# Rows of the experts' weights read in pairs, score products by turns on the two halves of TensorE's rows, and two more places for weights in each experts' stage

## The chip, the cores and the metric

One core of one Trainium2 chip. The time is device microseconds of one execution; runs are told as a median with the lowest and the highest. Smaller is better. All data are float32; matmuls take float32 or the fp32r type, and TensorE's two clock levels are 2.4 GHz (a granted clock of 1.00 in the views) and 1.2 GHz (0.50).

## The reference

The kernel computes a first block (a Fourier and state-space mixer over 256 tokens and 256 context tokens) and then two layers of a second block, on tokens of width 1024. Cut to what the change touches:

```python
for l in range(2):
    sh1, sc1, g1, sh2, sc2, g2 = split(silu(c) @ ada_w[l] + ada_b[l], 6)   # the same for the context from c_ctx
    h = rms_norm(x, norm_mix[l]) * (1 + sc1) + sh1
    # l == 0: even_layer (4 heads of differential attention, 8 of neighbourhood attention with a bias, all 64 wide)
    # l == 1: odd_layer  (8 heads of latent attention, 4 heads of retention in both directions)
    y, yc = layer(h, hc)
    x = x + g1 * y
    h2 = rms_norm(x, norm_ffn[l]) * (1 + sc2) + sh2
    x = x + g2 * expert_choice_ffn(h2, moe_router[l], moe_w1[l], moe_w3[l], moe_w2[l])
    # in layer 0 the context tokens go through the same experts' stage

def expert_choice_ffn(h, w_router, w1, w3, w2):        # 16 experts, width 1024, hidden width 1024
    aff = softmax(h @ w_router)
    gate, idx = top_k(swapaxes(aff, 1, 2), 32)          # each expert takes 32 of 256 tokens
    xe = h[bidx, idx]
    hid = silu(xe @ w1) * (xe @ w3)
    ye = (hid @ w2) * gate
    return zeros_like(h).at[bidx, idx].add(ye)
```

The three matrices of an expert are 4 MiB each, 192 MiB per layer, and each is used once.

## The kernel before, in words

One program runs the stages one after the other; inside a stage a scheduler decides the order of instructions on each engine from the order in which generators emit them (`weave` interleaves two generators, for instance one that attends with one that projects).

**The experts' stage** (`moe`, its `run` at the end of each layer). For expert `e`, `ffn` multiplies the 32 (layer 1) or 64 (layer 0: 32 of x and 32 of the context) chosen tokens by `moe_w1`, `moe_w3` and, after `silu` and a product, `moe_w2`. Each matrix comes as four loads of 1 MiB, each issued by SyncE (SP) in `load_m` (line 1253): a load takes 256 rows of the matrix, that is two blocks of 128 along the contraction, into a tile `wm` of 128 partitions by 2048 values. Partition p gets row p of the first block and row p of the second, two runs of 4 KB that lie 512 KB apart in HBM:

```python
w = pool.tile([128, 2048], F32, name="wm", tag=tag).rearrange("p (k n) -> p k n", k=2)
sv = src.rearrange("(k p) n -> p k n", p=128)
nc.sync.dma_start(w, sv[:, k0:k0 + 2])
```

The place of a load comes from a list, `slots`: a first round (`first`, which also holds places that are needed later for gathered tokens, the `xf` tiles) and then `all`, over and over. In layer 0 `all` has 16 places and the first round 20; in layer 1 they are 20 and 22. Places called `wx` come from the pools `mx0` (2), `mx1` (6) and others. A load into a place waits for the last matmul that read what was there; SP issues loads in order, so all later loads wait with it.

**The contraction's order.** Block k of the contraction holds channels 128k to 128k+127 everywhere: in the gathered tokens (`gather`: a product of the tokens' columns `xp` with a matrix `P` of zeros and ones), in the transposes of `hid` for the third matrix, in the transposes in `route` that feed the router, in the router's rows (`router_rows`), in the modulation columns (`ada`, sections 6 to 9, whose results are turned into columns) and in the columns of `norm_ffn_2` and `ada_b_2`.

**The scores.** In `even_attend` a score product contracts over 64 values, so it uses one half of TensorE's 128 rows: the two halves of a head pair lie on partitions 0 to 63 and 64 to 127. `scores` emits one head's products into one PSUM bank; with a bias (neighbourhood attention) the bias is added by a product of full height with a constant matrix `flipm`, behind the first score product. `retention` has three such groups: the state (`rv,kw`, 64 columns wide), the scores (`rqT,rkT`) and the cross term (`sst,rqT`). In the views line 149 is the helper that issues all matmuls, line 256 the one that transposes by a matmul with `kb`'s identity.

**Memory.** `kb` holds constants (identity, `tri`, `flipm`, `iota1`), `CV` columns and, later, the router's rows and affinities. POOL's own DMA descriptors have an area of 16384 bytes per partition.

Of the kernel before, what the change touches and what calls it, by code (L numbers as in the profile page):

```python
# [27 lines left out]
OP = mybir.AluOpType  # L28
# [8 lines left out]
def _constants():  # L37
# [9 lines left out]
    base = np.concatenate([ident, tri.reshape(128, 512), flip, iota1], 1)  # L47
# [45 lines left out]
    even = np.concatenate([np.tile(c64, (2, 1)), np.tile(s64, (2, 1)), perm, na.reshape(128, 128)], 1)  # L93
# [20 lines left out]
def kernel(ctx, tc, A, out, dbg=None):  # L114
# [130 lines left out]
    kb = pers.tile([128, 800], F32, name="kb")  # L245
    ident = kb[:, 0:128]
    tri = kb[:, 128:640].rearrange("p (a b) -> p a b", a=4)
    flipm = kb[:, 640:768]
    iota1 = kb[:, 768:800]
# [14 lines left out]
    CV = pers.tile([128, 200], F32, name="CV")  # L264
# [12 lines left out]
    hT = [htp.tile([128, 8, 512], F32R, name=f"hT{i}") for i in range(2)]  # L277
    pro = ExitStack()
# [4 lines left out]
    v4 = pp.tile([128, 128], F32, name="v4")  # L283

# [55 lines left out]

    def vcol(name, i):
        c = VCI[name] + i
        return VC[:, c:c + 1]
# [14 lines left out]

    def ada(src, s, pair, cols, bias, between=None, bank=None, ws=None):

        p = (bank or psa)()
        for b in range(2):
# [149 lines left out]
    with tc.issue_after(after):  # L512
        late_rows()
    now(c2)
# [539 lines left out]
    AFF = [CV[:, 128 + 32 * s:160 + 32 * s].rearrange("p (t e) -> p t e", t=2) for s in range(2)]  # L1054
    RW = [CV[:, 0:128].rearrange("p (k n) -> p k n", k=8), RWC]

    def router_rows(l):
        nc.sync.dma_start(RW[l], A["moe_router_2"][l].rearrange("(k p) n -> p k n", p=128))
# [22 lines left out]
    def route(l, s, src, at="a", tag="b", jt="b"):  # L1081
# [62 lines left out]
    def moe(l, streams, stk):  # L1144
# [42 lines left out]
        def gather(s, part, k, n=1):  # L1187
# [3 lines left out]
            if k % n == 0:  # L1191
                c = slice(128 * k, 128 * k + 128 * n)
# [49 lines left out]
        def load_m(src, k0, apart=False):  # L1242
# [5 lines left out]
            sv = src.rearrange("(k p) n -> p k n", p=128)  # L1248
            if apart:
                for k in range(2):  # L1250
                    nc.sync.dma_start(w[:, k], sv[:, k0 + k])
            else:
                nc.sync.dma_start(w, sv[:, k0:k0 + 2])
# [578 lines left out]
```

## Time and profile before

| | |
|---|---|
| time, median of 3 runs | 1906.96 us (1906.41 to 1912.91) |
| the profiled execution's own time | 1906.99 us |
| its span, first to last instruction | 1905.1 us (1.9 us lie around it) |
| mean granted clock of TensorE | 0.922 |
| busy: TensorE, VectorE, ScalarE, GpSimd | 1652.3, 794.4, 519.3, 335.1 us |
| loads of experts' weights | 382 of 1024 KB, median 18.4 us from issue to landing |

The span is the time from the first to the last instruction; what follows refers to microseconds from its start. A busy TensorE (PE) is not one at its peak, since matmuls are pipelined and their ends are modelled. The "DMA share" of a window is the mean busy share of the core's 16 DMA engines (packets that overlap make it a little over 1), GB/s what they moved. The chain of waits goes back from the last instruction to what released each step.

### The profile page before, as it was taken

The numbers are of one execution on the slowest core, as the hardware profiler recorded it, in microseconds if no ns is written. First come the engines' busy times: TensorE is split into PE (matmuls) and PEld (weight loads), VectorE is DVE, ScalarE is ACT, GpSimd is POOL, SyncE is SP. The second block draws the span as 40 slices with busy tenths as digits, with TensorE's granted clock in tenths as the row PEclk, the third lists the DMA queues.
The fourth block names the chain that finished last, engine by engine and source line by source line (L and its number), as shares of the span: only waits on it lengthen the run. The fifth ranks groups of instructions, "written<-read, shape, count | busy, mean of one in ns | idle before, by whom it ended". The sixth has DMA issues, their size and how long they took to land.

```text
span 1905.1 us, 29062 instructions
## 1 busy us (share of the span) xinstructions
PE 1652.3 (87%) x12036; PEld 1026.2 (54%) x12036; DVE 794.4 (42%) x1563; ACT 519.3 (27%) x1042; POOL 335.1 (18%) x288
## 2 busy tenths in 40 slices
PE   5999999899999998999989997789998966666665
PEld 4877777799887676433323322278784522222221
DVE  4538798947546655322323121164743300000002
ACT  4335555636443442211200000062532200000001
POOL 3114553633413310000000000041300000000001
PEclk8999999999999999999999999999997976776767
DMA  9576544555576539899989999951397999999996
GB/s 343 198 233 219 173 148 141 170 190 190 186 235 168 187 139 382 300 373 409 409 338 409 409 409 409 402 163 71 126 352 273 408 408 409 409 409 409 409 409 274
DMA packets 223016, 557.11 MB, mean 292 GB/s; under 512 B 23531, under 2 KB 80199, under 8 KB 222884
## 3 DMA queue, kind: packets, MB, share of 16 engines
q1 hardware_dynamic: 216608, 547.92, 76.9%
q10 hardware_dynamic: 5732, 6.26, 1.0%
q8 instruction: 95, 1.56, 0.3%
q0 software_dynamic: 544, 1.06, 0.1%
q14 instruction: 37, 0.30, 0.0%
HBM read 554.16 MB, written 1.05 MB: 291 GB/s over the span
## 4 chain that ended last, share of the span: by engine, by line
PE 60%; DMA 26%; DVE 8%; ACT 3%; issue 2%; POOL 1%; SPq 0%; DVEq 0%; POOLq 0%; ACTq 0%
PE ps_a L149 48%; DMA wm<-in_moe_w_dram 22%; PE ps_b L149 7%; PE ps_b L256 3%; DMA w<-in_w_in_dram 2%; DVE w L800 1%; PE ps_g L149 1%; DMA w<-in_w_ada_dram 1%; DVE wh L205 1%; ACT wh L203 1%; DMA w<-in_w_out_dram 1%; DVE ye L1323 1%; DVE pr L1404 1%; DVE hid L1305 1%; DVE acc L614 1%
## 5 line engine op out<-in xcount | busy, mean ns | idle before, releaser
L149 PE MATMUL ps_a<-wm,xf 128*32 128x256 f32 (+1 forms) x1792 | 280.0, 558 | 73.6 <-DMA wm<-in_moe_w_dram 71.8
L149 PE MATMUL ps_a<-wm,hidT 128*32 128x256 f32 (+1 forms) x1536 | 211.8, 529 | 47.4 <-DMA wm<-in_moe_w_dram 31.7
L149 PEld LDWEIGHTS ps_a<-wm,xf 128*32 128x32 f32 (+1 forms) x1792 | 90.4, 138 | 255.9 <-issue 133.3
L203 ACT ACTIVATE wh<-w 128x1024 fp32r<-128x1024 f32 (+3 forms) x152 | 151.7, 1007 | 164.6 <-PE ps_a L149 99.9
L1305 DVE TENSOR_TENSOR hid<-hid,ps_a 128x512 f32<-128x512 f32 (+1 forms) x32 | 17.7, 555 | 375.2 <-PE ps_a L149 375.2
L205 POOL TENSOR_TENSOR wh<-w,wh 128x1024 fp32r<-128x1024 f32 (+3 forms) x50 | 116.0, 2321 | 304.4 <-ACT wh L203 278.5
L205 DVE TENSOR_TENSOR wh<-w,wh 128x1024 fp32r<-128x1024 f32 (+3 forms) x102 | 135.2, 1329 | 71.9 <-ACT wh L203 71.4
L149 PEld LDWEIGHTS ps_a<-wm,hidT 128*32 128x32 f32 (+1 forms) x1536 | 70.4, 133 | 158.6 <-issue 74.8
L1323 DVE TENSOR_TENSOR ye<-ps_a,SC 32x512 f32<-32x512 f32 (+1 forms) x128 | 70.8, 553 | 193.9 <-PE ps_a L149 192.3
L1303 ACT ACTIVATE hid<-ps_a 128x512 f32<-128x512 f32 (+1 forms) x32 | 15.7, 490 | 480.9 <-PE ps_a L149 458.8
L149 PE MATMUL ps_a<-hT,wh 128*128 128x512 f32 (+1 forms) x672 | 136.3, 359 | 6.6 <-ACT hT L496 5.0
L1222 POOL TENSOR_TENSOR Pg<-Pg,CV 128x128 f32<-128x128 f32 x24 | 9.5, 421 | 748.7 <-DVE Pg L1220 748.7
L149 PEld LDWEIGHTS ps_a<-hT,wh 128*128 128x128 f32 x672 | 110.9, 197 | 25.9 <-ACT hT L496 5.4
L149 PE MATMUL ps_a<-E,wh 128*128 128x256 f32 x768 | 102.3, 288 | 6.1 <-DVE wh L205 2.5
L149 PE MATMUL ps_a<-wm,xe 128*32 128x256 f32 (+1 forms) x768 | 104.3, 481 | 0.7 <-ACT hid L1303 0.5
L149 PEld LDWEIGHTS ps_a<-E,wh 128*128 128x128 f32 x768 | 95.1, 192 | 12.6 <-issue 3.2
L149 PE MATMUL ps_a<-wh,E 128*128 128x256 f32 (+1 forms) x576 | 100.9, 326 | 0.1
L149 PEld LDWEIGHTS ps_a<-wh,E 128*128 128x128 f32 x576 | 81.5, 188 | 12.6 <-issue 5.0
L149 PE MATMUL ps_a<-wm,ye 128*32 128x256 f32 x512 | 51.6, 543 | 25.5 <-DMA wm<-in_moe_w_dram 25.5
L614 DVE SCALAR_TENSOR_TENSOR acc<-ps_a,CV,acc 128x189 f32<-128x189 f32 (+2 forms) x160 | 66.7, 427 | 8.2 <-ACT acc L603 5.7
L1023 ACT ACTIVATE pr<-ps_a,nb 128x512 f32<-128x512 f32 (+1 forms) x80 | 48.0, 601 | 76.0 <-DVE nb L1020 63.8
L149 PE MATMUL ps_a<-w,SC 128*32 128x128 f32 x1728 | 64.4, 281 | 2.7 <-DMA w<-in_w_ada_dram 2.1
(525 smaller groups left out, 2416.4 us busy)
## 6 DMA issues: line engine op xcount, KB each, us to landing
wm<-in_moe_w_dram SPq DMA_DIRECT2D x382, 1024.0 KB, 18.4
w<-in_ada_w_dram SPq DMA_DIRECT2D x46, 1024.0 KB, 5.8
w<-in_even_w_in_dram SPq DMA_DIRECT2D x24, 1024.0 KB, 6.4
w<-in_w_ada_dram SPq DMA_DIRECT2D x12, 1024.0 KB, 8.9
w<-in_w_in_dram SPq DMA_DIRECT2D x8, 1024.0 KB, 7.4
w<-in_even_w_out_dram SPq DMA_DIRECT2D x8, 1024.0 KB, 6.8
w<-in_w_in_dram SPq DMA_DIRECT2D x12, 512.0 KB, 7.3
w<-in_w_in_dram SPq DMA_DIRECT2D x8, 768.0 KB, 4.4
```

The source lines that it names most:

```text
L149: PE.matmul(o, l, r, start=start, stop=stop, **kw)
L203: S.activation(hv, wv, AF.Copy)
L205: (G if flip_lo[0] == 0 else V).tensor_tensor(lo, wv, hv, op=OP.subtract)
L256: PE.transpose(o, i, ident[:n, :n])
L614: V.scalar_tensor_tensor(o, xi[:, r0 + dr:r1 + dr, c0 + dc:c1 + dc], tap(i, j), o, op0=OP.mult, op1=OP.add)
L800: V.scalar_tensor_tensor(w[:, r], cb[:, c, 1], dt[:, c, 24 + h:25 + h], w[:, r], op0=OP.mult, op1=OP.add)
L1023: S.activation(pr[:, :n], ps[:, :n], AF.Exp, bias=nb, scale=scale, accum_out=su)
L1222: G.tensor_tensor(g_, g_, bcast(AFF[s][:, t, e4, None], [128, 4, 32]), op=OP.mult)
L1303: S.activation(hid, p1[:, :N], AF.Silu)
L1305: V.tensor_tensor(hid, hid, p3[:, :N], op=OP.mult)
L1323: V.tensor_tensor(ye[o:o + 32, s, N * j:N * j + N], py[i:i + 32, :N], G2[i:i + 32, :], op=OP.mult)
L1404: V.scalar_tensor_tensor(pr[0][0][:, :n], pr[1][0][:, :n], rc, pr[0][0][:, :n], op0=OP.mult, op1=OP.add)
```

## The change

1. **Rows in pairs.** A load of 256 rows now gives partition p rows 2p and 2p+1 of the 256: one run of 8 KB in HBM. Block k of the contraction so holds every second channel (`in_pairs`). Everything on the contraction's side follows: the transposes in `route` and of `hid`, the gathered columns (read with a step of 2 where `xp` is made, in layer 1, or where it is used as stationary operand, in layer 0), the moving operand of `ada` in sections 6 to 9, the router's rows and the columns of `norm_ffn_2` and `ada_b_2` (a new function `pair_rows`: three more DMAs on POOL, two transposes, three copies on VectorE).
2. **Two more places** in each experts' stage: `mx0` has 4 instead of 2, `mx1` 8 instead of 6, so `all` has 18 and 22 places and the first rounds 22 and 24. Room for them comes from the descriptor area (1024 instead of 16384 bytes per partition); besides, `CV` moves to the pool of `hT`, `flipm` from `kb` to `ke`, the affinities to `BC` and the first router's rows to `tri`.
3. **Scores by turns.** `scores` emits both halves of a head pair in turn, into two PSUM banks, the biases first; the three groups of `retention` go by turns on the halves too.

```diff
-            sv = src.rearrange("(k p) n -> p k n", p=128)
+            sv = src.rearrange("(m p i) n -> p m i n", p=128, i=2)[:, k0 // 2]
...
-                nc.sync.dma_start(w, sv[:, k0:k0 + 2])
+                nc.sync.dma_start(w, sv)
...
+    def in_pairs(j, n=128):
+        c = 256 * (j // 2) + j % 2
+        return slice(c, c + 2 * n - 1, 2)
...
+    def pair_rows():
+        ab = A["ada_b_2"]
+        ab = ab if len(ab.shape) == 2 else ab.rearrange("o l n -> (o l) n")
+        for l in range(2):
+            rows_in(v5, 8 * l, ab[l:l + 1, 3072:5120].rearrange("o (m c) -> (o m) c", c=256))
+        rows_in(v5, 16, A["norm_ffn_2"].rearrange("l (m c) -> (l m) c", c=256))
+        p = psb()
+        for i in range(2):
+            tr(p[:, 24 * i:24 * i + 24], v5[:, i::2])
...
-                    mm(p[32 * j:32 * j + 32, 0:128], SC[:, 4 * b + k, pair, :], w[:, k, 128 * j:128 * j + 128],
+                    mm(p[32 * j:32 * j + 32, 0:128], SC[:, 4 * b + k, pair, :],
+                       w[:, k, in_pairs(j) if paired else slice(128 * j, 128 * j + 128)],
...
-                tr(p[:, 256 * j + 128 * t:256 * j + 128 * t + 128],
-                   src[:, t, (2 * kk + j) * 128:(2 * kk + j + 1) * 128])
+                tr(p[:, 256 * j + 128 * t:256 * j + 128 * t + 128], src[:, t, in_pairs(2 * kk + j)])
...
-                    c = 128 * (k % n)
-                    mm(ps, pair[s][i][:, t, c:c + 128], Ps[s][:, t], start=t == 0 and i == 0, stop=t == 1 and i == 1)
+                    c = slice(0, 128) if n == 1 else in_pairs(k % n)
+                    mm(ps, pair[s][i][:, t, c], Ps[s][:, t], start=t == 0 and i == 0, stop=t == 1 and i == 1)
...
-                    tr(pt[:, 128 * c:128 * c + 128], hid[:, 128 * c:128 * c + 128])
+                    tr(pt[:, 128 * c:128 * c + 128], hid[:, in_pairs(c)])
...
-        def scores(ps, kind, ch, half, qs, bias=None):
-            hs_ = slice(64 * half, 64 * half + 64)
+        def scores(kind, ch, qs, bias=None):
+            pss = [psa(), psa()]
+            hs_ = [slice(64 * c, 64 * c + 64) for c in range(2)]
+            for c in range(2 if bias is not None else 0):
+                mm(pss[c][:, 0:256], flipm, bias[c], stop=False)
             for i, kv in enumerate(KVs):
-                b = bias is not None and i == 0
-                o = ps[:, 256 * i:256 * i + 256]
-                mm(o, Q[hs_, 4 * kind + ch, qs], kv[hs_, kind, 256 * ch:256 * ch + 256], stop=not b)
-                if b:
-                    mm(o, flipm, bias, start=False)
+                for c in range(2):
+                    mm(pss[c][:, 256 * i:256 * i + 256], Q[hs_[c], 4 * kind + ch, qs],
+                       kv[hs_[c], kind, 256 * ch:256 * ch + 256], start=i > 0 or bias is None)
+            return pss
...
-        for h in range(4):
-            o, a_ = slice(64 * (h % 2), 64 * (h % 2) + 64), h // 2
-            ps = psa()
+        for a_ in range(2):
+            pss = [psa(), psa()]
             for j in range(2):
-                mm(ps[:, 256 * j:256 * j + 256], rkT[o, a_, 128 * j:128 * j + 128], rqT[o, a_, :])
-            V.tensor_tensor(D[:, h], ps, D[:, h], op=OP.mult)
-            yield
+                for par in range(2):
+                    o = slice(64 * par, 64 * par + 64)
+                    mm(pss[par][:, 256 * j:256 * j + 256], rkT[o, a_, 128 * j:128 * j + 128], rqT[o, a_, :])
...
-    mx = enter(ms, name="mx0", bufs=2, reuse_waits="tile")
+    mx = enter(ms, name="mx0", bufs=4, reuse_waits="tile")
...
-    mx = enter(ms, name="mx1", bufs=6, reuse_waits="tile")
+    mx = enter(ms, name="mx1", bufs=8, reuse_waits="tile")
...
-    nc = _bacc.Bacc("TRN2", target_bir_lowering=False, num_devices=1)
+    nc = _bacc.Bacc("TRN2", target_bir_lowering=False, num_devices=1, dynamic_dma_scratch_size=1024)
```

Three places of the instructions' order. First SP's queue from where the first experts' stage is loaded (`wm<-in_moe_w_2_dram` is a load of 1 MiB of experts' weights, `kb<-in_moe_router_dram` the second layer's router, `in_ada_w_dram` modulation weights), as a difference of the two:

```order
-L1253 DMA wm<-in_moe_w_2_dram 128x2x1024 x6
-L1058 DMA kb<-in_moe_router_dram 128x8x16
-L1253 DMA wm<-in_moe_w_2_dram 128x2x1024
+L1279 DMA wm<-in_moe_w_2_dram 128x2048 x8
+L1085 DMA kb<-in_moe_router_dram 128x4x32
+L1279 DMA wm<-in_moe_w_2_dram 128x2048
 L189 DMA w<-in_ada_w_dram 128x4x512 x2
-L1253 DMA wm<-in_moe_w_2_dram 128x2x1024 x183
-L1251 DMA wm<-in_moe_w_2_dram 128x1024 x2
+L1279 DMA wm<-in_moe_w_2_dram 128x2048 x181
+L1277 DMA wm<-in_moe_w_2_dram 128x1024 x2
```

Eight instead of six loads stand ahead of the router's rows, 181 instead of 183 behind the last modulation weights, and each is one run per partition where it was two.

Second PE's queue in the neighbourhood attention of x (`KV,Q` is a score product on one half of the rows, `nb_t,kb` and `nb_t,ke` the bias product on all rows, `kb,pr` transposes of the probabilities). Before:

```order
L149 MATMUL ps_a<-KV,Q 128x256
L149 MATMUL ps_a<-nb_t,kb 128x256
L256 MATMUL ps_b<-kb,pr 128x128 x4
L149 MATMUL ps_a<-KV,Q 128x256 x2
L149 MATMUL ps_a<-nb_t,kb 128x256
L149 MATMUL ps_a<-KV,Q 128x256
```

After:

```order
L149 MATMUL ps_a<-nb_t,ke 128x256
L149 MATMUL ps_a<-KV,Q 128x256 x2
L255 MATMUL ps_b<-kb,pr 128x128 x4
L149 MATMUL ps_a<-nb_t,ke 128x256
L149 MATMUL ps_a<-KV,Q 128x256 x2
```

The bias now comes ahead of a head's two score products, which follow each other; both lie on the same half.

Third PE's queue at the context's attention, which is woven into projections of x (`E,wh`; the products `Q,ke` turn queries, `KV,prT` apply probabilities). Before, one of the single score products:

```order
L149 MATMUL ps_a<-KV,Q 128x256
L256 MATMUL ps_b<-kb,pr 128x128 x2
L149 MATMUL ps_a<-E_4479,wh 128x256
L149 MATMUL ps_a<-E_4480,wh 128x256
L149 MATMUL ps_a<-E_4479,wh 128x256 x2
```

After, one of the pairs:

```order
L149 MATMUL ps_a<-E_4489,wh 128x256
L149 MATMUL ps_a<-KV,Q 128x256 x2
L149 MATMUL ps_a<-E_4489,wh 128x256
L149 MATMUL ps_a<-E_4490,wh 128x256
L149 MATMUL ps_a<-E_4489,wh 128x256 x2
```

In this stretch 32 score products stood in 25 places of the queue; now they stand in 18, of which 14 are a product on the lower half and one on the upper half side by side.

## Rows read from the trace of the kernel before

**Rows 1.** The span in 40 equal slices: GB/s moved by DMA

```profile
GB/s 343 198 233 219 173 148 141 170 190 190 186 235 168 187 139 382 300 373 409 409 338 409 409 409 409 402 163 71 126 352 273 408 408 409 409 409 409 409 409 274
```

**Rows 2.** The chain that ended last, shares of the span

```profile
PE 60%; DMA 26%; DVE 8%; ACT 3%; issue 2%; POOL 1%; SPq 0%; DVEq 0%; POOLq 0%; ACTq 0%
PE ps_a L149 48%; DMA wm<-in_moe_w_dram 22%; PE ps_b L149 7%; PE ps_b L256 3%; DMA w<-in_w_in_dram 2%; DVE w L800 1%; PE ps_g L149 1%; DMA w<-in_w_ada_dram 1%; DVE wh L205 1%; ACT wh L203 1%; DMA w<-in_w_out_dram 1%; DVE ye L1323 1%; DVE pr L1404 1%; DVE hid L1305 1%; DVE acc L614 1%
```

**Rows 3.** Stages: length, busy us (xcount) by engine, clock, DMA share, GB/s

```profile
467.00:590.00 123.00, 121.70 (x1182) 104.33 (x1182) 61.61 (x157) 52.48 (x133) 41.25 (x42) 1.00 0.62 201
592.00:735.00 143.00, 139.44 (x899) 103.80 (x898) 93.63 (x193) 59.81 (x135) 40.65 (x34) 0.99 0.57 186
982.00:1237.00 255.00, 222.88 (x964) 72.22 (x960) 49.09 (x79) 8.96 (x15) 4.83 (x12) 1.00 1.03 408
957.00:982.00 25.00, 21.15 (x87) 7.11 (x89) 6.61 (x12) 1.19 (x2) 0.00 (x0) 0.86 0.71 277
1340.00:1372.00 32.00, 31.82 (x216) 23.92 (x215) 22.55 (x37) 13.84 (x32) 15.93 (x17) 1.00 0.20 68
1437.00:1453.00 16.00, 15.44 (x96) 9.46 (x100) 5.48 (x12) 4.82 (x9) 2.09 (x2) 0.50 0.43 136
1459.00:1889.00 430.00, 301.15 (x3095) 121.22 (x3090) 52.92 (x133) 24.06 (x60) 3.66 (x9) 0.75 1.02 407
```

**Rows 4.** SP's waits, 790 to 1090 us: total, times, longest

```profile
SPq L1253 <- PE ps_a L149: 199.4, 95, 18.3
```

**Rows 5.** PE's waits for weights, 1095 to 1240 us: total, times, longest

```profile
PE ps_a L149 <- DMA wm<-in_moe_w_dram: 17.0, 26, 1.2
```

**Rows 6.** The same, 1459 to 1889 us

```profile
PE ps_a L149 <- DMA wm<-in_moe_w_dram: 112.0, 117, 2.9
```

**Rows 7.** PE's timeline, scores: start us, us, engine, line, operation, count

```profile
473.71 0.70 PE L149 MATMUL ps_a<-KV,Q 64*128 64x256 f32 x4
...
496.32 0.70 PE L149 MATMUL ps_a<-KV,Q 64*128 64x256 f32 x2
...
623.03 0.70 PE L149 MATMUL ps_a<-KV,Q 64*128 64x256 f32 x2
623.66 0.70 PE L149 MATMUL ps_a<-nb_t,kb 128*128 128x256 f32 x2
...
655.37 1.14 PE L149 MATMUL ps_a<-KV,Q 64*128 64x256 f32 x8
```

**Rows 8.** PE's timeline, retention's state and first scores

```profile
1346.12 2.57 PE L149 MATMUL ps_a<-rv,kw 128*64 128x128 f32 x32
1348.62 1.13 PE L149 MATMUL ps_a<-rqT,rkT 64*128 64x256 f32 x4
```

**Rows 9.** POOL's timeline, a DMA of the late rows

```profile
20.22 0.51 POOL L287 DMA_DIRECT2D v<-in_norm_ffn_dram  x1
```

**Rows 10.** Weight loads of TensorE by tile: busy us, mean ns

```profile
L149 PEld LDWEIGHTS ps_a<-P,xp 128*128 128x128 f32 x128 | 19.9, 224 | 13.9 <-issue 10.6 <-ACT xp L1201 1.4 <-ACT xf L163 0.8
L256 PEld LDWEIGHTS ps_t<-kb,hid 128*128 128x128 f32 x64 | 6.7, 141 | 19.7 <-DVE hid L1305 19.7
```

**Rows 11.** DMA, 350 to 354 us, rows of 1 KB: packets, MB, share

```profile
q1 hardware_dynamic: 1444, 1.46, 109.6%
```

**Rows 12.** DMA, 327 to 331 us, rows of 2 KB

```profile
q1 hardware_dynamic: 805, 1.62, 105.1%
```

**Rows 13.** DMA, 1040 to 1060 us, rows of 4 KB

```profile
q1 hardware_dynamic: 2121, 8.19, 102.6%
```

**Rows 14.** DMA queues of instruction packets, whole span: packets, MB, share

```profile
q8 instruction: 95, 1.56, 0.3%
q14 instruction: 37, 0.30, 0.0%
```

**Rows 15.** DMA, 1560 to 1564 us, one instruction packet

```profile
q14 instruction: 1, 0.01, 0.5%
```

**Rows 16.** DMA, 960 to 964 us, one instruction packet

```profile
q8 instruction: 1, 0.02, 1.5%
```

More of the change, by code (lines that the diff above doesn't have):

```diff
@@ L277 @@
     hT = [htp.tile([128, 8, 512], F32R, name=f"hT{i}") for i in range(2)]
+    CV = htp.tile([128, 200], F32, name="CV")
     pro = ExitStack()
@@ L283 @@
     v4 = pp.tile([128, 128], F32, name="v4")
+    v5 = pp.tile([24, 256], F32, name="v5")
     def rows_in(t, r0, ap, eng=G):
@@ L357, in ada_early @@
             early[l, s].append(w)
+    def in_pairs(j, n=128):
+        c = 256 * (j // 2) + j % 2
+        return slice(c, c + 2 * n - 1, 2)
     def ada(src, s, pair, cols, bias, between=None, bank=None, ws=None):
         p = (bank or psa)()
+        paired = pair == 1 and 6 <= s < 10
         for b in range(2):
@@ L1344 @@
     l3 = enter(el3, name="el3", bufs=1, reuse_waits="tile")
-    ke = l2.tile([128, 768], F32, name="ke")
+    ke = l2.tile([128, 896], F32, name="ke")
     S.dma_start(ke, A["k_even"])
@@ L1393, in even_attend @@
             for h in range(4):
-                pr = []
-                for c in range(2):
-                    ps = psa()
-                    scores(ps, 0, h, c, qs)
-                    pr.append(softmax_p(l2, ps, n, 1.0, "pr"))
+                pr = [softmax_p(l2, ps, n, 1.0, "pr") for ps in scores(0, h, qs)]
                 rc = sm.tile([128, 1], F32, name="rc", bufs=6)
@@ L1417, in even_attend @@
             su8 = sm.tile([128, 8], F32, name="su8")
-            for h in range(8):
-                ps = psa()
-                scores(ps, 1, h // 2, h % 2, qs, None if nb_t is None else nb_t[:, t, h])
-                pr, su = softmax_p(l2, ps, n, 1.0, "pr")
-                G.tensor_copy(su8[:, h:h + 1], su)
-                values(po[:, 64 * h:64 * h + 64], transposed(l2, pr, nk), 1, 64 * h)
-                yield
+            for hh in range(4):
+                prs = [softmax_p(l2, ps, n, 1.0, "pr")
+                       for ps in scores(1, hh, qs, None if nb_t is None else [nb_t[:, t, 2 * hh + c] for c in range(2)])]
+                for c, (pr, su) in enumerate(prs):
+                    h = 2 * hh + c
+                    G.tensor_copy(su8[:, h:h + 1], su)
+                    values(po[:, 64 * h:64 * h + 64], transposed(l2, pr, nk), 1, 64 * h)
+                    yield
             V.reciprocal(su8, su8)
@@ L1714, in retention @@
             cr = rs_.tile([128, 2, 2, 2, 128], F32, name="cr")
[L1715 to L1721 removed]
+            pss = [psa(), psa()]
+            for a_ in range(2):
+                for d in range(2):
+                    c = 128 * (2 * d + a_)
+                    for par in range(2):
+                        o = slice(64 * par, 64 * par + 64)
+                        mm(pss[par][:, c:c + 128], rqT[o, a_, qs], sst[o, d, a_, :])
+            for par in range(2):
+                ps = pss[par]
                 dq = dec[:, 0, t].rearrange("p d (a b) -> p d a b", b=2)[:, :, :, par, None]
@@ L1780 @@
     x3 = enter(x3s, name="x3b", bufs=2, side="right", reuse_waits="tile")
[L1781 removed]
+    slots["all"] += [(mx, "wx")] * 8 + [(ml, "wx")] * 4 + [(hring, "wh"), (hring, "wi")] * 2 + [(ring, "w")] * 4 + [(x3, "wx")] * 2
     slots["first"] += slots["all"]
```

52 lines of the change are left out of this document (26 added, 26 removed).

## The prediction

> **What bounds the kernel now.** I read the chain of waits first [rows 2]: 60% of the span hangs on TensorE (PE) and 26% on DMA, of which 22%, some 420 us, are loads of experts' weights. Then GB/s by slices [rows 1]: two flat stretches at 409 between lower values, so weights come at one constant rate there, while elsewhere DMA has room. The windows by stage [rows 3] say what each stage waits for. The attention stretches (467 to 590 and 592 to 735 us) have PE busy for 99% and 98% of the time with DMA at 0.62 and 0.57: every PE microsecond saved there ends the stage earlier. From 982 to 1237 us and from 1459 to 1889 us DMA's share is 1.03 and 1.02: there only fewer or cheaper packets help, or loads that have landed before. That PE has room is seen in its waits for weights: 17.0 us at the end of the first experts' stage [rows 5], 112.0 us in the second [rows 6]. A load of 1 MiB costs 2.56 us there (8.19 MB in 20 us, [rows 13]).
>
> Ahead of both stretches lies a gap in DMA: 0.71 from 957 to 982 us, 0.43 from 1437 to 1453 us [rows 3]. SP then waits for PE to give a place back: 199.4 us in 95 waits between 790 and 1090 us [rows 4]. So the last load ends, in both stages, at "when DMA resumes, plus 2.56 us for each load still to come".
>
> **The change part by part.**
>
> *Places.* With two more, the load that goes out into a given freed place is two further on in the list, so when DMA resumes two loads fewer are left. The gaps have room for them: 0.29 of 25 us is 7.3 us, 0.57 of 16 us is 9.1 us, and two loads take 5.1 us. So -5.1 us in each stage, -10.2 us. Below, nothing, if another wait takes the gap; above, 9.1 us in the second stage.
>
> *Rows in pairs.* A load moves the same bytes in half as many data packets, 8 instead of 16 per DMA engine. No row shows an 8 KB packet of this queue, so I bound its price from three sides. First, shorter rows of the same queue, as busy time of 16 engines per packet's bytes: 1 KB took 1.096 x 64 us / 1.46 MB, 0.049 us [rows 11]; 2 KB took 0.085 us [rows 12]; 4 KB took 0.164 us [rows 13]. Two halves cost more than the whole by 2 x 0.049 - 0.085 = 0.013 us, and by 2 x 0.085 - 0.164 = 0.006 us. An 8 KB packet should then cost 0.328 us less 6 to 13 ns; I take 8 ns, close to the nearer pair, so 8 x 8 = 64 ns per load. Second, no gain at all, if a long run is cut into pieces of 4 KB. Third, instruction packets: those of q14 hold 8 KB each (0.30 MB in 37, [rows 14]) and one took 0.5% of 64 us, 0.32 us, by rounding 0.29 to 0.35 [rows 15], on both sides of 0.328; those of q8 hold 16 KB and one took 1.5%, 0.96 us [rows 16], against 0.656 for four of 4 KB. By their name these carry instructions, not tiles, so I go by the queue's own rows. Loads that gain: 255 us / 2.56, less the two, some 98 in the first stage (-6.3 us), and 430 / 2.56 less two, 166, in the second (-10.6 us); -16.9 us. Bounds: 0 and -27 us for 13 ns, and a loss, below. PE's 17.0 us of waiting in the first stage [rows 5] cover the 11.4 us that DMA gives up there.
>
> The Trainium skill ("DMA: Bandwidth & Descriptors", section "Why small descriptors are slow") puts a fixed cost of about 3 cycles on each packet, beside one cycle per 32 bytes. By that, an estimate, two packets of 131 cycles become one of 259, 1.1% of 2.56 us or 0.03 us per load, and the sum would be 9 us smaller in gain (1883 us). The rows above give 2.5% and decide here.
>
> *Scores of the context* (467 to 590 us). A product is two records. One on one half alone (x2 at 496.32 us) and two on different halves side by side (x4 at 473.71) both show 0.70 us [rows 7], of which 0.63 pass until the successor starts (623.03 to 623.66): the second is free. The queue has 18 such places instead of 25: -7 x 0.63 = -4.4 us, on a stage that is PE's. Bounds -6 and 0 (if softmax becomes late: two heads' scores now need two PSUM banks at once).
>
> *Scores of x* (592 to 735 us). Neighbourhood attention stood as score, bias, score: 3 x 0.63 = 1.88 us [rows 7]. Two products on one half, beside two on the other, take 1.14 us shown, 1.07 to the successor (x8 at 655.37), so a further product of 256 columns adds 0.43 to 0.63, and each change between half and full height costs the other 0.2 us. Bias, score, score has one change less, 1.68 us. But where before both heads stood together (score, bias, two scores side by side, bias, score: 5 x 0.63 = 3.14 us), the new order on the same half gives 2 x 1.68 = 3.36 us. By the order, summed over the 16 heads and the differential scores, I get 39.0 us before and 38.3 us now: -0.7 us, bounds -3 and +1.
>
> *Retention.* Two score products on the same half show 1.13 us [rows 8], 1.06 to the successor, four times; now there are two runs of four on both halves, 1.07 each [rows 7]: -2.1 us. The 16 state products took 2.57 us [rows 8]; of 128 columns each, half of 0.43 us, eight pairs by turns take 1.7: -0.8 us. The cross term, nothing. The stage is PE's to 99% [rows 3], but the chain there also passes VectorE, so -2.5 us; bounds -3 and 0.
>
> *What is added.* Three DMAs on POOL, 0.51 us each [rows 9], behind work that nothing waits for; two transposes and three small copies before the layers start, +0.6 us if they lie in the open. Strided operands: the transposes in `route` (48), of `hid` (96) and the stationary `xp` (192) now read every second value, as do 256 products in `ada`. Weight loads take 0.141 us (transposes) and 0.224 us (`P,xp`) [rows 10]. I take +1 us in all, since weight loads run beside matmuls; bounds 0 and the doubling of a rival below. The router's rows are requested earlier on SP, and their wait for PE is no later than the neighbours'; nothing. The smaller descriptor area concerns POOL's DMAs alone, which are few and early; nothing, or an issue's 0.51 us where one waits for room.
>
> **Sum**: -10.2 - 16.9 - 4.4 - 0.7 - 2.5 + 0.6 + 1.0 = -33.1 us against the profiled execution's 1906.99 us (its span 1905.1 us and 1.9 around), which is the median of 1906.96 but for 0.03. **Forecast 1874 us.**
>
> **Rivals.**
>
> *The long run brings no rate* (cut into 4 KB, or the engines' rate is the same at 8 KB). For it: from 2 to 4 KB the saving was already half of that from 1 to 2 KB [rows 11 to 13]. Then -16.2 us remain: 1891 us.
>
> *The places bring nothing*, because the first loads only fill earlier and a later wait for PE opens the same gap. Against it: the shares of 0.71 and 0.43. 1884 us.
>
> *Strided reads cost double.* If a stationary operand with a step of two loads at half speed, 48 route transposes at 0.141 us cost 6.8 us in PE's stretches, the gathers ahead of the second stage's first product (32 at 0.224) 7.2 us, and the `hid` and `xp` loads while PE is behind in the first stage (40 x 0.141 + 64 x 0.2 = 18.4 us until 1095 us, of which some 60% before the gap at 957 to 982 us) 11 us more of gap: 1899 us. Against it: a float32 column takes four cycles of the engine (256 in 0.43 us at 2.4 GHz), so there is time for it. The Trainium skill ("SBUF — State Buffer", section "Specifications (TRN2)") says that reads are free as long as each 16-byte line is hit at least twice and that each step to a new line costs something; a step of two float32 hits each line twice, the very limit, and no row of before shows such an operand on PE.
>
> *The long packet is slower* (the other side). One mechanism: an 8 KB packet costs an engine more than two of 4 KB. Places and PE's gains without packets are 16.2 us, and 264 loads of 8 packets pay for it, so the sum is zero at 7.7 ns over 0.328 us, 0.336 us. At the upper end of q14's row, 0.35 us, the loss is 264 x 8 x 0.022 = 46 us, net 1937 us; at q8's price per byte it would be hundreds. For it: q8's row, and that q14's is not below 0.328 for certain [rows 15, 16].
>
> **How the numbers follow.** All as forecast 0.65; no rate 0.17; strided reads 0.06; places nothing 0.05; slower packet 0.07. The first case alone runs from 1860 us (13 ns, 6 us in the context's scores, 3 in x) to 1882 us (attention stretches give nothing); 4 us more from the second stage's gap make the lower end 1856. The range 1856 to 1896 us also takes in "no rate" and "places nothing"; it leaves out the slower packet, most of strided reads and the tails, 0.16. A measurement tells about 0.5% from no change, 9.5 us, so faster means under 1897.4 us: the first, second and fourth case and part of the third, 0.90; within 0.5%, the rest of the third and a slight loss by packets, 0.04; slower 0.06.
>
> **What would show it.** Pairing: a queue of hardware packets with some 48,000 fewer, DMA's share in the flat stretches unchanged at 1.02 to 1.03, GB/s up from 408 to about 418, 2.50 us per load; no gain if GB/s stays, slower if it falls under 400. Places: the share in the gaps nearer to 1, and load 90 where load 88 went out. Scores: the context's stretch shorter by 4 us, x's by less than 1, retention's by 2. Strided reads: mean weight-load times of `kb,hid` and `xp` above 0.141 and 0.224 us. The forecast is wrong if the flat stretches keep 408 GB/s, or if PE's waits for weights in the first stage vanish, which would make PE its bound.

## The result, and the profile after

The changed kernel takes 1881.5 us, the median of 4 runs (1879.19 to 1888.28), the kernel before, beside it, 1909.93 us (4 runs, 1906.41 to 1915.25). The ratio is 0.9855, 95% interval [0.9816, 0.9894]: faster by 1.5%, some 28 us, where 33 were forecast. The profiled execution took 1879.31 us with a span of 1877.3 us, 27.8 us less than before.

The slices of GB/s first, which answer to [rows 1]:

```profile
GB/s 348 189 223 232 167 143 145 201 152 212 179 233 169 228 125 396 313 352 420 421 269 420 421 421 421 420 214 78 68 362 271 423 425 425 425 425 425 425 424 261
```

Both flat stretches are higher than 409, but not by the same: 421 in the first, 425 in the second. The dips ahead of them are still there (269 in the slice that begins at 939 us). The chain still has 59% PE and 27% DMA, so nothing new has become the bound.

The windows by stage (columns as in [rows 3]), with the places of each stage in the new trace:

```profile
468.00:589.00 121.00, 118.78 (x1195) 104.75 (x1195) 63.60 (x159) 51.70 (x136) 40.45 (x42) 0.99 0.62 206
589.00:728.00 139.00, 136.39 (x911) 105.32 (x911) 86.71 (x190) 58.98 (x135) 40.99 (x36) 0.99 0.60 206
967.00:1226.00 259.00, 236.76 (x1026) 82.08 (x1022) 49.78 (x80) 10.15 (x17) 4.86 (x12) 0.99 1.01 418
951.00:966.00 15.00, 11.14 (x36) 4.70 (x36) 11.67 (x22) 3.02 (x8) 0.00 (x0) 0.76 0.04 8
1427.00:1443.00 16.00, 15.17 (x96) 9.24 (x99) 5.46 (x13) 4.81 (x9) 2.03 (x2) 0.51 0.39 132
1449.00:1859.00 410.00, 290.52 (x3098) 121.74 (x3090) 52.93 (x133) 23.90 (x60) 3.69 (x9) 0.79 1.01 422
```

The gap ahead of the first flat stretch did not close, it got deeper: DMA at 0.04 for 15 us, 14.4 us of its time lost where 7.3 were before (0.29 of 25 us [rows 3]), with TensorE's granted clock at 0.76 in it. PE's waits for weights, the counterparts of [rows 5] (1090 to 1228 us) and [rows 6] (1449 to 1859 us):

```profile
PE ps_a L149 <- DMA wm<-in_moe_w_dram: 5.6, 11, 0.6
```

```profile
PE ps_a L149 <- DMA wm<-in_moe_w_dram: 101.2, 106, 1.7
```

At the end of the first experts' stage PE hardly waits any more: 5.6 instead of 17.0 us.

Where the 27.8 us came from, by the start of the first score product, of the first and the last product on experts' weights of each stage, and the end, in PE's timelines of the two profiles:

| stretch | before, us | after, us | difference | forecast |
|---|---|---|---|---|
| start to first score of the context | 467.4 | 468.3 | +0.9 | +0.6 |
| to the first product on layer 0's experts | 296.4 | 290.9 | -5.5 | -5.1, and +1.0 for strides |
| first experts' stage | 473.4 | 466.9 | -6.5 | -11.4 |
| to the first product on layer 1's experts | 202.3 | 203.8 | +1.5 | -2.5 |
| second experts' stage | 451.2 | 431.4 | -19.8 | -15.7 |
| to the end | 14.5 | 16.1 | +1.6 | 0 |

The runs of one kernel differ by some 10 us, and in the fourteen profiles of this study the first stretch alone, which the change hardly touches, is between 467.4 and 473.3 us long. So the experiments below are read by their medians and, for the cause, by the length of these stretches. The last row's +1.6 goes with PE's clock: in the chain that ended last the closing sums took 4.52 us for six records in a window with a granted clock of 0.76, where four took 1.97. It is not the change: a second profile of the changed kernel, below, has 14.5 us there, as the kernel before.

### The profile page after: what moved, and what is told of

Its sections match the earlier page's. It is cut to its first block, busy times and chain, and to the rows that moved or that the text cites. A ratio compares the mean times of both kernels' runs of the same rounds, so it can differ in the third digit from the quotient of the medians.

```text
span 1877.3 us, 29103 instructions
## 1 busy us (share of the span) xinstructions
PE 1642.5 (87%) x12038; PEld 1039.4 (55%) x12038; DVE 788.9 (42%) x1566; ACT 517.8 (28%) x1042; POOL 335.3 (18%) x291
## 4 chain that ended last, share of the span: by engine, by line
PE 59%; DMA 27%; DVE 7%; ACT 3%; issue 2%; POOL 1%; SPq 0%; DVEq 0%; POOLq 0%; ACTq 0%
PE ps_a L149 47%; DMA wm<-in_moe_w_dram 22%; PE ps_b L149 7%; PE ps_b L255 3%; DMA w<-in_w_in_dram 2%; PE ps_g L149 1%; DVE w L827 1%; DMA w<-in_even_w_in_dram 1%; DMA w<-in_w_ada_dram 1%; ACT wh L203 1%; DVE wh L205 1%; DMA w<-in_even_w_out_dram 1%; DVE ye L1349 1%; DVE hid L1331 1%; PE ps_t L255 1%
## 5 line engine op out<-in xcount | busy, mean ns | idle before, releaser
L149 PE MATMUL ps_a<-wm,hidT 128*32 128x256 f32 (+1 forms) x1536 | 207.2, 509 | 42.0 <-DMA wm<-in_moe_w_dram 25.3
L1248 POOL TENSOR_TENSOR Pg<-Pg,BC 128x128 f32<-128x128 f32 x24 | 9.5, 422 | 735.1 <-DVE Pg L1246 735.1
L1329 ACT ACTIVATE hid<-ps_a 128x512 f32<-128x512 f32 (+1 forms) x32 | 15.7, 490 | 448.8 <-PE ps_a L149 448.8
L149 PE MATMUL ps_a<-wm,ye 128*32 128x256 f32 x512 | 45.4, 498 | 23.0 <-DMA wm<-in_moe_w_dram 23.0
```

What stands on the lines that cost most here:

```text
L149: PE.matmul(o, l, r, start=start, stop=stop, **kw)
L1248: G.tensor_tensor(g_, g_, bcast(AFF[s][:, t, e4, None], [128, 4, 32]), op=OP.mult)
L1329: S.activation(hid, p1[:, :N], AF.Silu)
```

## The experiments

The changed kernel was taken apart, one part undone at a time, and then the two surprises (the unequal rates, the deeper gap) were followed. Ratios are against the kernel before, with 95% intervals.

**Rows of 4 KB again.** All operands at a step of one, places and turns as changed:

```diff
-            sv = src.rearrange("(m p i) n -> p m i n", p=128, i=2)[:, k0 // 2]
+            sv = src.rearrange("(k p) n -> p k n", p=128)[:, k0:k0 + 2]
...
-        c = 256 * (j // 2) + j % 2
-        return slice(c, c + 2 * n - 1, 2)
+        return slice(128 * j, 128 * j + n)
...
-        pair_rows()
```

> The change with part 1 undone: rows of 4 KB as before, all operands at a step of one; places and turns as changed. Theory (the long packet): an 8 KB packet takes 0.310 us where two of 4 KB took 0.328, so GB/s in the flat stretches falls back from 421 and 425 to 408 to 410, the second experts' stage is longer by 166 x 0.096 = 16 us and the first by some 5 (there PE's waits for weights go back up from 5.6 to 12 or more); 1900 us, 1896 to 1905. Rival (the rate came from the places or the higher granted clock, not from the packets): GB/s stays above 418, 1881 us.

1890.69 us, ratio 0.9894 [0.9877, 0.9912]; stages 472.5 and 438.4 us. Theory and rival both miss. The first stage is back to 409 GB/s and 5.6 us longer, as the theory says, but the second stays at 417 with rows of 4 KB and is 7.0 us longer instead of 16. The DMA view of this kernel, 1600 to 1700 us (packets, MB, share):

```profile
q1 hardware_dynamic: 10782, 41.58, 102.2%
```

and the same of the kernel before and of the changed one:

```profile
q1 hardware_dynamic: 10578, 40.77, 102.2%
```

```profile
q1 hardware_dynamic: 5829, 42.47, 100.9%
```

By bytes, as in the prediction, 4 KB take 1.022 x 1600 us / 41.58 MB, 0.161 us, where before they took 0.164, and 8 KB take 0.311. So the long run saves 11 ns against two short ones of the same kernel (0.322), and another 6 ns came from something that this experiment had not undone. Per load that is 2.515 us (417 GB/s) to 2.461 (426), 54 ns, close to the forecast's 64; the other 49 ns (409 to 417) had no term.

**Two places fewer.** 2 and 6 again, all else as changed:

```diff
-    mx = enter(ms, name="mx0", bufs=4, reuse_waits="tile")
+    mx = enter(ms, name="mx0", bufs=2, reuse_waits="tile")
...
-    mx = enter(ms, name="mx1", bufs=8, reuse_waits="tile")
+    mx = enter(ms, name="mx1", bufs=6, reuse_waits="tile")
```

> The change with part 2 undone: 2 and 6 places again, all else as changed. Theory (each place one load ahead when DMA resumes): the second stage ends 5 us later counted from its start, the first 0 to 5 us later (PE there waits only 5.6 us for weights); 1884 to 1890 us. Rival (the places only fill earlier, a later wait for PE takes the gain): 1881 us, with the same end of both stages.

1893.19 us, ratio 0.991 [0.9892, 0.9928]; stages 467.3 and 435.8 us. The whole time lies above the theory's 1884 to 1890, but in its profile the first stretch, which places hardly touch, is 5.0 us longer than in the changed kernel. The second stage loses 4.4 us, two loads nearly as forecast. The first loses nothing (467.3 against 466.9): there the two places bring nothing in the changed kernel. Why, PE's queue shows. Every trace in which the gathers go through one buffer has one stretch without products on weights near 950 us: the sums of the first quarter of the experts (`ye,PgT`) overwrite x, so the last gathers of x (`P,xp`) have to come first. The groups of PE's products there, with two places fewer (945.7 to 962.0 us; matmul records, busy us, mean ns, idle before):

```profile
L149 PE MATMUL ps_g<-P,xp 128*128 128x256 f32 x24 | 6.9, 393 | 2.8 <-DVE xp L1228 1.8 <-ACT xp L1227 0.9
L149 PE MATMUL ps_b<-ye,PgT 128*128 128x512 f32 x10 | 5.5, 634 | 1.3 <-DVE x L1361 1.1 <-DVE xc L1361 0.2
```

and in the changed kernel (941.4 to 961.5 us):

```profile
L149 PE MATMUL ps_g<-P,xp 128*128 128x256 f32 x28 | 9.6, 439 | 3.3 <-DVE xp L1228 1.8 <-ACT xp L1227 1.4
L149 PE MATMUL ps_b<-ye,PgT 128*128 128x512 f32 x10 | 6.8, 761 | 0.9 <-DVE x L1361 0.5 <-DVE xc L1361 0.2
```

With more places the scheduler puts products on weights earlier and leaves one gather more, 28 products for 24, to this break. From the last product on weights ahead of it to the next one it is 19.0 us long instead of 15.6, in the kernel before 15.6 as well. Load 90 waits for a place that comes back behind the break, and goes out at 964.5 us, where load 88 of the kernel before went out at 963.7: two loads further, but from a PE that had been 4.7 us ahead. Counted from the stage's first product on weights, load 88 goes out at 199.9 us in the kernel before and at 200.2 us with two places fewer, load 90 in the changed kernel at 205.4 us. That is 5.2 us later, as long as two loads take (2.49 us each at 421 GB/s), so the gain is gone. Only a part of the longer break is the gather itself: the old order of scores, next, has the same 28 products there at 376 ns instead of 439 and a break of 17.2 us; the rest goes with the lower clock.

**Scores in the old order**, all else as changed (the old loops of `even_attend` and `retention` put back):

```diff
-                for c in range(2):
-                    mm(pss[c][:, 256 * i:256 * i + 256], Q[hs_[c], 4 * kind + ch, qs],
-                       kv[hs_[c], kind, 256 * ch:256 * ch + 256], start=i > 0 or bias is None)
+                b = bias is not None and i == 0
+                o = ps[:, 256 * i:256 * i + 256]
+                mm(o, Q[hs_, 4 * kind + ch, qs], kv[hs_, kind, 256 * ch:256 * ch + 256], stop=not b)
+                if b:
+                    mm(o, flipm, bias, start=False)
```

> The change with part 3 undone: scores and retention in the order of before, all else as changed. Theory (PE's saving passes through): the first product with experts' weights starts 5 to 7 us later than 759.1 us and the end is 5 to 7 us later, 1886 us. Rival (the lead is given back in the first experts' stage, whose end is set by DMA or by PE's own work there): the start of that stage is later, its end by less than 2 us, 1881 us.

1887.85 us (1879.86 to 1890.16), ratio 0.9869 [0.9849, 0.9889]. The profiles are clearer than the medians: from the first to the last score 234.8 us here, 225.5 in the changed kernel, and the two experts' stages no longer (464.2 and 431.3). The first of these is 2.7 us shorter than in the changed kernel, so part of the lead is given back there, as the rival has it, and the rest of some 9 us passes through; by the whole times it is not shown, since their intervals overlap. The retention's stretch, from its first state product to the latent attention's last score, is the same to 0.1 us with and without turns (40.7 us in the kernel before, 40.6 in both others).

**Every operand at a step of one**, with the long rows kept:

```diff
-        c = 256 * (j // 2) + j % 2
-        return slice(c, c + 2 * n - 1, 2)
+        return slice(128 * j, 128 * j + n)
```

> The change with the weights' rows in pairs, but every operand on the contraction's side read at a step of one (route's and hid's transposes, xp, ada), so channels meet the wrong rows of the weights and router: what is left out is the matching order. It prices the strided reads alone. Theory (weight loads run beside matmuls): transposes' weight loads go back from 0.207 to 0.141 us, time by 0 to 2 us, 1879 to 1881 us. Rival (the strided loads ate PE's lead in the first experts' stage): that stage's PE work is 4 to 5 us shorter, 1875 to 1877 us.

1882.03 us (1874.84 to 1882.33), ratio 0.9837 [0.9818, 0.9857]; stages 466.4 and 432.1 us. Weight loads of TensorE by tile, the changed kernel first, then this one:

```profile
L149 PEld LDWEIGHTS ps_a<-P,xp 128*128 128x128 f32 x128 | 20.7, 230 | 14.2 <-issue 11.4 <-ACT xp L1227 1.4 <-ACT xf L163 0.8
L255 PEld LDWEIGHTS ps_t<-kb,hid 128*128 128x128 f32 x64 | 8.9, 207 | 19.8 <-DVE hid L1331 19.8
```

```profile
L149 PEld LDWEIGHTS ps_a<-P,xp 128*128 128x128 f32 x128 | 19.8, 224 | 13.9 <-issue 10.6 <-ACT xp L1226 1.4 <-ACT xf L163 0.8
L255 PEld LDWEIGHTS ps_t<-kb,hid 128*128 128x128 f32 x64 | 6.7, 140 | 19.8 <-DVE hid L1330 19.8
```

A stationary operand read at a step of two loads in 0.207 instead of 0.140 us in the transposes, 0.230 instead of 0.224 with layer 1's `xp`. The two experts' stages are as long without it as with it, within 0.7 us; the loads are hidden, as the theory says.

**The changed kernel again, and its addresses.** What else had moved with the change is where the places lie. In the built programs all 22 places of the second stage of the kernel before start at 32 bytes beyond a multiple of 64 within a partition; with the smaller constants and the new places 22 of 24 start at a multiple. Four kernels on one chip: the changed one, one with two paddings that align the other places too, one with a padding of 32 bytes at the left end (no place of the second stage aligned), and, for the scores, one that keeps the turns:

> The changed kernel itself, as the reference for the runs beside it: about 0.9855 of the kernel before, 1879 to 1886 us, 421 GB/s in the first flat stretch and 425 in the second.

1884.26 us, ratio 0.9868 [0.9845, 0.989]; stages 466.5 and 430.0 us.

```diff
+    enter(name="padr", bufs=1, side="right").tile([128, 8], F32, name="padr")
     htp = enter(hts, name="hTp", bufs=1, side="right", reuse_waits="tile")
...
-    subl = l1.tile([128, 1], F32, name="subl")
+    subl = l1.tile([128, 16], F32, name="subl")[:, 0:1]
```

> The change with two paddings of 32 bytes per partition (a tile at the right end, and subl 64 instead of 4 bytes), so that all places for weights start at a multiple of 64 bytes; before, every place of the second stage lay at 32 beyond one, in the change 2 of 22 there and 10 of 18 in the first stage. Theory (a place's address sets the packet's time): 8 KB packets take 0.310 us in both stages, the first stage reads 425 GB/s instead of 421, the second 426; time 0 to 3 us less, as PE waits only 5.6 us for weights at the first stage's end. Rival (the first stage is slower for another reason, such as PE's own traffic): 421 there as before.

1878.08 us, ratio 0.9835 [0.9818, 0.9852]; stages 465.7 and 429.5 us, 421 and 425 GB/s. In the first stage the rival holds: nothing changes there. The lower median is not seen in the stages and not told from the changed kernel's.

```diff
     pers = enter(name="pers", bufs=1)
+    pers.tile([128, 8], F32, name="padl")
```

> The change with one padding of 32 bytes per partition at the left end, so that all places of the second stage start at 32 beyond a multiple of 64 bytes, as in the kernel before. Theory (address): the second stage falls from 425 to about 421 GB/s and 0.314 us per 8 KB packet, 4 us longer. Rival (the smaller descriptor area, or fewer bytes elsewhere, made the second stage's rate): 425 stays, same time.

1888.91 us, ratio 0.9887 [0.9873, 0.9902]; stages 467.7 and 434.7 us. The DMA view of 1600 to 1700 us:

```profile
q1 hardware_dynamic: 5747, 41.88, 100.9%
```

1.009 x 1600 us / 41.88 MB is 0.316 us for 8 KB where the changed kernel takes 0.311, 420 GB/s for 425, and the stage is 4.7 us longer than that of the changed kernel beside it (430.0) and at least 2.6 us longer than in the ten profiles with long rows, all places and no such shift (429.5 to 432.1). A shift of the tiles at the left end by 32 bytes is all that differs, so addresses do set the second stage's rate, by 5 ns per 8 KB packet here. Between the kernel before and the one with its rows apart it is 3 ns per 4 KB packet, but other things differ between those two as well.

A multiple of 64 is not the whole rule. GB/s of the kernel with rows of 4 KB, 1600 to 1700 us, in slices of 2.5 us, about one load each:

```profile
GB/s 406 410 413 408 413 424 423 410 421 421 423 421 421 423 408 419 423 421 423 411 408 410 406 410 410 410 419 419 419 424 408 419 419 419 421 419 421 426 413 419
```

Of a round of 22 loads some seven in a row stay at 406 to 411, about the rate of the kernel before, though two of the 22 places alone lie off a multiple of 64. What sets those apart is not shown.

```diff
+            last = None
             for c in range(2 if bias is not None else 0):
-                mm(pss[c][:, 0:256], flipm, bias[c], stop=False)
+                last = PE.matmul(pss[c][:, 0:256], flipm, bias[c], start=True, stop=False)
             for i, kv in enumerate(KVs):
+                with tc.issue_after(last.ins) if last is not None else ExitStack():
...
+                last = now_
```

> The change with an order kept on PE in the scores: both biases first, then the first score products of both halves, then the second ones, each behind the one before; in the change the scheduler put both products of one half together in x's attention. Theory (two halves side by side cost as one): 8 pairs of neighbourhood heads at 2.1 instead of 3.2 us, the stretch to the last score of x 7 to 9 us shorter, end of the kernel 4 to 8 us earlier. Rival (softmax of both heads then waits together, so PE idles instead): the stretch not shorter, PE's share in it lower, 0 to 2 us.

1892.0 us, ratio 0.9907 [0.9889, 0.9925], by the medians 7.7 us slower than the changed kernel beside it, with intervals that just touch. x's stretch is longer, not shorter. The windows from the end of the projections that are woven into the context's attention to the last score, the changed kernel and this one:

```profile
566.70:693.80 127.10, 124.57 (x923) 95.31 (x924) 75.16 (x162) 53.59 (x129) 42.34 (x38) 0.99 0.55 178
```

```profile
566.70:700.90 134.20, 123.39 (x916) 94.68 (x916) 73.25 (x160) 52.65 (x127) 41.91 (x37) 0.91 0.53 168
```

PE's work is 1.2 us less, but it has 10.8 us of idle time for 2.5, and a clock of 0.91. PE's waits in this kernel's window:

```profile
PE ps_a L149 <- ACT wh L203: 5.0, 1, 5.0
PE ps_b L255 <- ACT pr L1050: 4.3, 3, 2.6
```

The rival holds in part: PE waits 4.3 us for softmax results (`pr`), which it did not in the changed kernel. As long is one wait for weights that ScalarE converts (`wh`), 5.0 us for 1.9; that ScalarE is late there because of the softmax of both heads is likely, but not shown. The theory's saving is there too: the scores and biases together keep PE busy for 37.0 us instead of 42.6. The products around them take longer at the lower clock.

**The break in PE's queue.** Gathers in the first stage go one by one through a single buffer `xp`. With two buffers (and one place less for their room), with two buffers and two places less, and with `xp` in the ring of four row buffers and all 18 places, each on top of the aligned kernel:

```diff
-                    xp = mp.tile([128, 2, 2, 128], F32R, name="xp")
+                    xp = mp.tile([128, 2, 2, 128], F32R, name="xp", bufs=2)
...
-    mx = enter(ms, name="mx0", bufs=4, reuse_waits="tile")
+    mx = enter(ms, name="mx0", bufs=3, reuse_waits="tile")
```

> The aligned kernel with two buffers for xp in the first experts' stage (its gathers there no longer follow one behind the other through one buffer) and 17 instead of 18 places to make room for it; all else as in the aligned kernel. In the change PE's queue has a break of 19 us at load 72, in which 28 gather products and 10 records of the first quarter's sums stand without any product on weights, since those sums overwrite x and must wait for the last gather; with 16 places it is 15.6 us and 24 products. Theory (that break sets when places come back, so two more places were paid for by a longer break): without it DMA does not fall to 0.05 at 951 to 966 us, the first stage is 7 to 10 us shorter from its first product to its last, 1868 to 1872 us. Rival (the stage is PE's by its products alone): 0 to 2 us shorter, 1877 us.

1873.23 us, ratio 0.9811 [0.979, 0.9832]; first stage 460.0 us, 5.7 less than in the aligned kernel (465.7): less than the theory's 7 to 10, more than the rival's 0 to 2. DMA does not fall at 951 to 966 us:

```profile
951.00:966.00 15.00, 13.40 (x64) 5.19 (x62) 0.69 (x1) 1.19 (x2) 0.00 (x0) 1.00 1.01 422
```

> The same with 16 places in the first stage, as in the kernel before. Theory: with the break gone, a place is worth at most one load of 2.49 us here, and nothing if DMA never has to wait; the first stage is 0 to 3 us longer than with 17. Rival (places are what matters): 5 us longer or more.

1874.98 us, ratio 0.9821 [0.9797, 0.9845]; first stage 464.8 us.

```diff
-                    xp = mp.tile([128, 2, 2, 128], F32R, name="xp")
+                    xp = rowp.tile([128, 512], F32R, name="xp", tag="r").rearrange("p (i t c) -> p i t c", i=2, t=2)
```

> The aligned kernel with xp in the ring of four row buffers (shared with hid and others) instead of its own single buffer, 18 places. The gathers are then done by load 44, in breaks of up to 36 products, ahead of the first sums. Theory: no break with sums and gathers together, so PE's order loses less than 5 us in breaks and the stage is 7 to 10 us shorter, as with two buffers; rival (hid waits for the shared buffers): the stage as long as in the change.

1869.91 us, ratio 0.9791 [0.9769, 0.9813], the lowest median here, though the intervals of the other two overlap with it; first stage 455.6 us, 10.1 less than in the aligned kernel. What was the gap of DMA, 951 to 966 us, is now (945 to 970 us):

```profile
945.00:970.00 25.00, 23.41 (x111) 8.98 (x109) 3.43 (x5) 1.19 (x2) 0.00 (x0) 1.00 1.02 422
```

DMA is busy throughout and PE's clock full. The longest stretch without products on weights behind 800 us is 8.6 us, of gathers alone, and 3.8 us with two buffers, where it was 19.0. So the break was what set when places came back. Without more places it is worth little: 464.8 us with two buffers and 16 places, 467.3 with one buffer and 16 places. The gain of 10.1 us needs both. A place is worth 4.8 us between the two kernels with two buffers by their profiles, 1.75 by their medians, whose intervals overlap: more than the theory's 3 by the one, within it by the other. The profile with 16 places is one of its slower runs (1879.26 us), so that stays open.

**All places at a multiple of 128 bytes**, for the first stage's rate, on top of the ring:

```diff
-    enter(name="padr", bufs=1, side="right").tile([128, 8], F32, name="padr")
+    enter(name="padr", bufs=1, side="right").tile([128, 24], F32, name="padr")
...
-    subl = l1.tile([128, 16], F32, name="subl")[:, 0:1]
+    subl = l1.tile([128, 32], F32, name="subl")[:, 0:1]
```

> The kernel with xp in the ring, with the two paddings enlarged to 96 and 128 bytes per partition, so that every place of both stages starts at a multiple of 128 bytes (in the aligned kernels the first stage's places lay at 64 beyond one, but for eight, the second stage's at a multiple, but for two); order of instructions unchanged. Theory (128 bytes is the step that decides): 8 KB packets in the first stage fall from 0.314 to 0.310 us, 425 GB/s there instead of 421, as in the second; PE's waits for weights there fall below 10 us and the time by 0 to 3 us, 1867 to 1870 us. Rival (the first stage is slower for another reason than address): 0.314 us and 421 GB/s stay.

1872.45 us, ratio 0.9799 [0.978, 0.9818]. The DMA view of 1100 to 1200 us, the changed kernel and this one:

```profile
q1 hardware_dynamic: 5770, 42.02, 101.1%
```

```profile
q1 hardware_dynamic: 5783, 42.10, 101.2%
```

Nothing changes: 0.315 us per 8 KB and 421 to 422 GB/s in the first stage at any address that was tried. What holds it there is open.

## Why the prediction was right, and where its terms were off

The time lies in the range and moved the way that was forecast. That the sum is off by no more than 5.3 us (27.8 for 33.1) is in part luck: the first experts' stage and retention's stretch gave 8.9 us less than forecast, and the second experts' stage gave 4.1 us more, in part by a cause for which the prediction had no term. By steps:

*Places, -5.1 us in each stage.* Right in the second stage (4.4 us). In the first the rival "the places bring nothing" held, in its own words: a later wait for PE opened the same gap. The step that failed is "the gaps have room for them". Room in DMA's gap was taken from the trace of before, with PE's order as it stood there, and the change's order has one gather more in the break. Where to read it is the order of PE's queue at the break itself. One of the prediction's own signs of being wrong also came near: of 17.0 us of waiting for weights in the first stage 5.6 are left.

*Rows in pairs, -16.9 us.* The size per load was near: 54 ns in the second stage against 64, and 67 ns (409 to 420 GB/s) with the places at 32 beyond a multiple of 64 as in the kernel before. By stages it is worth 5.6 (472.5 to 466.9) and 7.0 us (438.4 to 431.4), 12.6 together, strided reads included, where places are as in the change. None of the instruction packets' rows [rows 14 to 16] bore on it. The Trainium skill's 3 cycles per packet ("DMA: Bandwidth & Descriptors", section "Why small descriptors are slow") would make, as an estimate, 0.03 us per load; here it is 0.05 to 0.07 (409 to 421 GB/s in the first stage is 73 ns, with strides and all).

*No term: the address of the places.* The second stage's 451.2 us became 431.4, 4.1 more than the 15.7 forecast. The kernel that is shifted back by 32 bytes shows what the two terms give at the addresses of before: 434.7 us, 16.5 less, nearly as forecast. The address then brings 3.3 to 4.7 us. Counted in the other order, places 4.4 and long rows 7.0 come last, and some 8 us (166 loads by 49 ns) are left for the address at rows of 4 KB. So long rows and addresses save in part the same time, and the two sizes can't be added. The prediction had "nothing" for the smaller descriptor area, and no word on where the tiles come to lie.

*Scores of the context, -4.4, and of x, -0.7.* The context's stretch, from its first score to the last of x's projections, went from 101.4 to 98.4 us. x's, from there to the last score, went from 131.1 to 127.1, far more than 0.7. PE's timeline of the changed kernel shows a group that was sized as 1.68 us:

```profile
640.36 0.60 PE L149 MATMUL ps_a<-nb_t,ke 128*128 128x256 f32 x2
640.89 1.13 PE L149 MATMUL ps_a<-KV,Q 64*128 64x256 f32 x4
641.95 0.65 PE L255 MATMUL ps_b<-kb,pr 128*128 128x128 f32 x4
```

Bias, score, score take 1.59 us, and elsewhere 1.68. Over 16 heads that is 1.5 us at most. Of the 4.0 us, 1.0 are fewer waits and 3.1 less work of PE (127.6 to 124.6 us busy): its score products take 2.3 us less (34.8 to 32.5) and the biases 1.1 (11.2 to 10.1). In part these are the context's own pairs, of which some stand behind this boundary. That the turns themselves were not kept in x was right, and the last experiment on them shows that keeping them would have cost, not saved.

*Retention, -2.5.* Nothing came. PE's work in the stretch fell from 40.5 to 39.0 us, but the stretch from 40.7 to 40.6: the step "the stage is PE's" was wrong. Once PE gives way it waits there, 1.1 us for softmax results (`pr`) and 0.5 for the copied state (`sst`). The stretch between the experts' stages even grew by 1.5 us, but the two profiles of the changed kernel alone differ by 2.4 there (203.8 and 206.2), so that growth is not told from their spread.

*Strided reads, +1.* The rows show the loads 47% longer (0.141 to 0.207 us) in the transposes, half of the way to the rival's doubling, and no stage that paid. The rival could not have come out as it was sized: it counts strided loads of `xp` in the first stage, but there all gathers behind the first quarter read `xp` densely, since the copy into it takes the step; it is layer 1, and layer 0's first quarter, where the stationary operand is strided (the list of the change has this the wrong way round). Over the first stage they took 0.209 us, and 0.211 with every step at one. The Trainium skill's limit of two hits per 16-byte line ("SBUF — State Buffer", section "Specifications (TRN2)") promises full bandwidth at two hits; here a load with exactly two was slower, and the measurement decides.

*A slower long packet* did not happen: 0.311 to 0.316 us is under 0.328 everywhere.

## What to carry to other kernels

Where a stage is DMA's at its end, ask what sets the moment at which DMA resumes: here a break in PE's queue with a serial chain through one buffer took all that two places for weights would have brought, and more buffers for that chain, with the places, were worth 10.1 us in that stage. When a change gives the scheduler more room, read its new order at the break itself, not only at the lines of the diff. When tiles move in memory, compare the start addresses of DMA's targets before crediting a new rate to the new access pattern.

## What was not expected of the hardware

The start of a DMA's target within a partition can matter: with all places at 32 beyond a multiple of 64 bytes runs of 8 KB took 0.316 us on average, with nearly all at a multiple 0.311, and a padding of 32 bytes alone made the rate 420 instead of 425 GB/s. Runs of 4 KB took 0.164 and 0.161 us, between kernels that differ in more. That held in the second experts' stage only, and not for all of its loads; in the first, 0.315 us and 421 GB/s stood at 32, 64 and 128 bytes alike.

A stationary operand of float32 at a step of two elements loads in 0.207 us where a dense one takes 0.140.
